# Decay products, norm spacing and tile loads in a conditioned hybrid decoder step

## The chip, the cores and the metric

The kernel runs on one core of one Trainium2 chip. The metric is the device time of one execution in microseconds (us), lower is better. Five engines share the work: TensorE (PE in the profile, matmuls, with its weight loads shown as PEld), VectorE (DVE), ScalarE (ACT), GpSimd (POOL) and SyncE (SP), which issues nearly all transfers. Every engine carries out its own list of instructions in order, and waits on semaphores for the others.

## The reference

One inference step of a two-layer decoder trunk, for a prompt of 1024 tokens and for 8 decoded tokens, with a model width of 1024. Every sub-layer has the same frame:

```
h = h + gate(c) * F(rmsnorm(h) * (1 + scale(c)) + shift(c))
```

`c` is a conditioning vector; scale, shift and gate come from a product with it. Layer 0 mixes with a gated linear recurrence (8 heads of 128 by 128 state, decay `f` per key channel and token), then has a SwiGLU feed-forward block of hidden width 2816:

```
q, f_raw, i, g = split(xn @ w_in, 4)
f = lb + (1 - lb) * sigmoid(f_raw);  k = 1 - f;  v = i
S_t = diag(f_t) S_(t-1) + k_t v_t^T;  o_t = q_t S_t
mix = (rmsnorm(o) * gnorm * silu(g)) @ w_o
```

Then one shared key and value projection is made from a norm of the residual stream. Layer 1 mixes with sliding-window attention (window 128, 16 query heads on 4 shared heads, sinks and a relative bias) and has a second feed-forward block. A last norm gives the output; the recurrent state and the key and value windows are outputs too.

## The kernel before, in words

Activations lie transposed, with the channels on the 128 partitions and 1032 tokens (1024 of the prompt and 8 decoded ones) along the free dimension, in 8 tiles of 128 channels. A product is made with float32 operands split in a high and a low part (three matmuls: high by high, high by low, low by high; L283 to L285). Tokens are cut into three chunks of 344 columns (`G3`) or four chunks of 258 (`G4`). The weights come by the SP queue into three `raw` buffers of 128 by 1024, are split by ScalarE (L182) and GpSimd (L185) into a ring of 8 halves, and `ws.next()` issues the loads of the units that follow within a look-ahead of six halves.

The order of instructions on each engine is not the order of the program. A planner takes instructions by priority, which is their place in the program, as soon as by its own estimate their inputs and a buffer are ready; one that is ready early can come ahead of others that were written earlier. `tc.keep_in_program_order(i)` adds one edge of order and no wait: `i` comes behind the instruction that was written before it for the same engine. Most SBUF tiles share one pool (`c4`) of 34 slots.

**The recurrence** (`hgrn_core`, one call a head). The decayed scores of a token block are built by doubling, at blocks of 1, 2, 4, 8, 16, 32 and 64 tokens. For each level TensorE makes 64 small matmuls of keys by queries (L1041; the two largest levels have lines of their own), and `double` on VectorE scales the second half of every block of queries (L1062) and the first half of the keys (L1063) with the decay of the other half, copies the level's scores under a mask (`take`, L1055), and multiplies the decays of neighbouring blocks (L1067) for the next level: 512 products on each partition at the first level, then 256, down to 8. L1062 and L1063 of one level must be done before L1041 of the next, and must themselves wait for their own level's L1041, which reads what they overwrite. L1067 reads and writes only the decays. `run` interleaves the core of one head with the projections of the next in the program, so large matmuls (L283 to L285) lie between the levels; L1003 and L1005 prepare the decays of the next head on VectorE.

**The norms.** The output projection of each mixer (`wo_second`) makes 8 products for each 258-column chunk; VectorE adds each to the residual stream (L842), ScalarE squares it, VectorE or GpSimd add the squares (L786). When a chunk is complete, a generator (`then`) is queued: `finish` merges the squares (L799), lets some steps pass, sums over the partitions with small matmuls (L712), makes the reciprocal root on VectorE with Newton steps (L543 to L552) and a diagonal tile (L718), lets some steps pass, broadcasts the root over the partitions with a matmul (L727) and copies it (L728). `apply_steps` scales (L807), modulates (ScalarE, L827) and splits (L834, L835) the normed activations. `step()` runs after every product and moves the queued generators on; a step with `LAG` costs nothing itself. After the last chunk, the steps come after the products of the feed-forward block, 24 matmuls each, and `need(x, c)` runs steps until a chunk is ready. The shared keys' norm (`ToKV`) does the same beside the last group of the first feed-forward block, in chunks of 344 columns.

**The feed-forward block** (`ffn`) makes the hidden tiles 0 to 21 and stores each to memory (`act_out`, L1510), most of them with a seven-product scheme whose 28 input tiles fill the pool. For the second matrix the hidden tiles are read back in groups: `hidden(j0, n)` loads n of them (L1517), casts the high part on ScalarE (L1518) and makes the low part on GpSimd and VectorE in turn (L1519). The first group has two tiles, the others four. The loads of the second group (tiles 2 to 5) are written after the products of the first group, and so after the `ws.next()` calls that issue weight loads (L195).

Of the kernel before, what the change touches and what calls it, by code (L numbers as in the profile page):

```python
# [12 lines left out]
ALU = mybir.AluOpType  # L13
# [40 lines left out]
G3, G4 = Grid(344), Grid(258)  # L54
# [3 lines left out]
def bc(ap, axis, n):  # L58
    u = ap.unsqueeze(axis)
    shape = list(u.shape)  # L60
    shape[axis] = n
    return u.to_broadcast(shape)
# [3 lines left out]
def trunk_kernel(  # L66
# [40 lines left out]
    pe, act, dve, pool, sp = nc.tensor, nc.scalar, nc.vector, nc.gpsimd, nc.sync  # L107
# [10 lines left out]
    def nm(s):  # L118
        uid[0] += 1
        return f"{s}_{uid[0]}"  # L120

    def big(dt=F32, cols=TOK, parts=P):
        return p4.tile([parts, cols], dt, tag="c4", name=nm("c4"))
# [11 lines left out]
    def axp():  # L135
        return pp.tile([P, 512], F32, tag="ax", name=nm("ax"), bufs=4)

    def small(shape, tag, bufs=2, dt=F32):
        return sm.tile(shape, dt, tag=tag, name=nm(tag), bufs=bufs)
# [266 lines left out]
    for kk in range(4):  # L406
        t = big(cols=1024)
        wa[0].append(first_half(2 * kk, 0, t))
        t = big(cols=1024)
        wa[0].append(first_half(2 * kk + 1, 0, t))  # L410
    ws.ahead(3)
    for k in range(4):
        t = big(cols=1024)
# [126 lines left out]
    def newton(y, ms, n, parts, tag):  # L540
        t = small([P, 12], tag + "t")[:, :n]
        tv, yv = t[:parts], y[:parts]
        dve.tensor_scalar(  # L543
            tv.bitcast(I32), ms.bitcast(I32), 1, None, op0=ALU.logical_shift_right
        )
        dve.tensor_scalar(
            yv.bitcast(I32), tv.bitcast(I32), -1, MAGIC, op0=ALU.mult, op1=ALU.add
        )
        for _ in range(3):
            dve.scalar_tensor_tensor(tv, yv, -0.5, yv, op0=ALU.mult, op1=ALU.mult)  # L550
            dve.tensor_tensor(tv, tv, ms, op=ALU.mult)
            dve.scalar_tensor_tensor(yv, tv, 1.5, yv, op0=ALU.add, op1=ALU.mult)  # L552
# [4 lines left out]
    def queue(g):  # L557


        later.append([g, next(g) == LAG])  # L560
# [119 lines left out]
    class Norm:  # L680
# [20 lines left out]
            for i in range(2):  # L701
                dve.tensor_reduce(self.acc[i][:, T:TOK], v[:, i], axis=AX.X, op=ALU.add)

        def finish(self, c):
            g = self.g
            s, n, w = g.all(c), g.nq, g.w
            self.merge(c)
            for _ in range(3):
                yield LAG
            ps = axp()  # L710
            for j in range(n):
                pe.matmul(ps[:Q, j : j + 1], self.sums(c, j), ones[:, 0:1], start=True, stop=True)  # L712
            ms = small([P, 12], "nms")
            y = small([P, 12], "ny")
            dve.tensor_scalar(ms[:Q, :n], ps[:Q, :n], 1.0 / D, EPS, op0=ALU.mult, op1=ALU.add)
            newton(y[:, :n], ms[:Q, :n], n, Q, "n")
            dg = small([P, W], "w", 6)[:, :w]
            dve.tensor_tensor(  # L718
                dg[:Q].rearrange("p (j q) -> p j q", j=n),
                bc(ident[:Q, :Q], 1, n),  # L720
                bc(y[:Q, :n], 2, Q),
                op=ALU.mult,
            )
            for _ in range(4):
                yield LAG
            ps = axp()
            pe.matmul(ps[:, :w], ones[:Q, :], dg[:Q], start=True, stop=True)  # L727
            act.copy(self.R[:, s], ps[:, :w])  # L728
# [119 lines left out]
    def residual_dec(tdec):  # L848
        dve.tensor_tensor(hd, hd, tdec, op=ALU.add)


    N = Norm()
# [34 lines left out]
    for half in range(2):  # L887
# [5 lines left out]
            op=ALU.mult,  # L893
# [115 lines left out]
    def hgrn_core(hh):  # L1009
# [6 lines left out]
        for half in range(2):  # L1016
            ps = axp()
            for j in range(4):
                c = 4 * half + j
# [37 lines left out]
        def double(M, pl, off, done=None):  # L1057
            nb = T // (2 * M)
            q4 = QP.rearrange("p (n two m) -> p n two m", two=2, m=M)
            k4 = KS.rearrange("p (n two m) -> p n two m", two=2, m=M)  # L1060
            p3 = pl.rearrange("p (n two) -> p n two", two=2)
            dve.tensor_tensor(q4[:, :, 1, :], q4[:, :, 1, :], bc(p3[:, :, 0], 2, M), op=ALU.mult)  # L1062
            dve.tensor_tensor(k4[:, :, 0, :], k4[:, :, 0, :], bc(p3[:, :, 1], 2, M), op=ALU.mult)  # L1063
            if done:
                take(*done)
            nxt = f[:, off : off + nb]
            dve.tensor_tensor(nxt, p3[:, :, 0], p3[:, :, 1], op=ALU.mult)  # L1067
            return nxt, off + nb

        psv = level(0)  # L1070
# [45 lines left out]
        for half in range(2):  # L1116
            ps = axp()
            for j in range(4):
                c = 4 * half + j
# [6 lines left out]
        for half in range(2):  # L1126
# [4 lines left out]
            for j in range(4):  # L1131
                c = 4 * half + j
# [25 lines left out]
        for half in range(2):  # L1158
            ps = axp()
            po.append(ps)  # L1160
            for j in range(4):
                c = 4 * half + j
                s = slice(c * P, (c + 1) * P)
                o = ps[:, j * P : (j + 1) * P]
# [3 lines left out]
            for j in range(4):  # L1168
                c = 4 * half + j
# [25 lines left out]
        for half in range(2):  # L1195
# [4 lines left out]
                op=ALU.mult,  # L1200
# [4 lines left out]
        for half in range(2):  # L1205
            ps = axp()
            for j in range(4):
                c = 4 * half + j
# [119 lines left out]
    def wo_second(o, gate, m, back, beside=iter(())):  # L1328
        tdec = small([P, KT, NB], "tdec", 2)
        us = [ws.next() for _ in range(4)]  # L1330
        st = res[-1]
        N = StackNorm(st)
        x = Quads()

        def then(c):
            st.move(back, [c], False)
            yield from N.finish(c)
            yield LAG
            yield from N.apply_steps(c, m, x)

        for c in range(G4.n):
            for n in range(KT):
                wo_product(us[n // 2], o, c, n, gate, tdec, G4, anyp)
                N.square(c, n)
                step()
                if c and ((c - 1) * KT + n) % 2 == 0:
                    next(beside, None)
            if c == G4.last:
                residual_dec(tdec)
                N.square_dec()  # L1350
            queue(then(c))
        for _ in beside:
            pass
        return x, st
# [64 lines left out]
    def ffn(l, x, st, hs, norm, aside=None):  # L1419

        gff = 48 * l + 40
        act_out = dp.tile([NF, P, TOK], F32, name=f"ff{l}")
# [87 lines left out]
            sp.dma_start(act_out[j], sg)  # L1510


        def hidden(j0, n, engines=(pool, dve)):
            o = Rows(n)
            for k, (xh, xl) in enumerate(o.t):
                t = big()
                sp.dma_start(t, act_out[j0 + k])  # L1517
                act.copy(xh, t)  # L1518
                engines[k % 2].tensor_tensor(xl, t, xh, op=ALU.subtract)  # L1519
            return o  # L1520
# [14 lines left out]
            seven_products(j, back if j == NF - 1 else None)  # L1535

        o = ready.pop()
        tdec = small([P, KT, NB], "tdec", 2)
        us = [ws.next() for _ in range(2)]
        for c in range(NCH):  # L1540
# [5 lines left out]
                residual(ps, c, n, gff, tdec)  # L1546
        residual_dec(tdec)
        for j0 in range(2, NF - 4, 4):
            o = hidden(j0, 4)
            tdec = small([P, KT, NB], "tdec", 2)  # L1550
            for np_ in range(4):
                u = ws.next()
                for c in range(NCH):
                    for n in (2 * np_, 2 * np_ + 1):
                        wo_product(u, o, c, n, gff, tdec)
            residual_dec(tdec)
        last = norm()
        o = hidden(NF - 4, 4)
# [19 lines left out]
    o = mixed(osc, 0)  # L1578
# [4 lines left out]
    o = mixed(osc, 1)  # L1583
# [6 lines left out]
    class ToKV(StackNorm):  # L1590
# [12 lines left out]

        def then(self, c):
            self.st.move(hsc, [c], False)
            yield from self.finish(c)
            yield LAG
            yield from self.apply_steps(c, 2, self.x, keep=True)

# [21 lines left out]
    for a in range(2):  # L1631
        t = big(cols=T)
# [257 lines left out]
    o = mixed(asc, 0)  # L1890
# [15 lines left out]
    o = mixed(asc, 1)  # L1906
# [137 lines left out]
```

## Time and profile before

| | us |
|---|---|
| median of 3 runs (2546.59 to 2551.95) | 2549.77 |
| the profiled execution | 2554.92 |
| its span, first to last instruction | 2553.1 |
| TensorE busy | 2481.1 |
| VectorE busy | 1370.6 |
| ScalarE busy | 877.9 |
| GpSimd busy | 777.0 |

The mean granted clock of TensorE is 0.988. A row of the waits names the engine and line that waited, then the one that ended the wait, the microseconds in total, how often, and the longest. A row of a timeline has the start in us, the duration, the engine, the line, what is written and read with its shape, the count of merged instructions, and in brackets the idle time of the engine ahead of it and what ended it. A row of grouped instructions has the count, the busy time in us and the mean of one in ns, and the idle time ahead. A row of a stretch has its bounds and length, the busy time of PE, PEld, DVE, ACT and POOL, then the granted clock, the busy share of the DMA engines and GB/s. A row of the chain of waits has start, duration and what it was.

### The profile page before, as it was taken

How to read it: one execution, taken by the hardware profiler on the slowest of the kernel's cores; microseconds unless marked ns; L12 is line 12 of the kernel's file. 1: busy time of each engine (PE TensorE's matmuls, PEld its weight loads, DVE VectorE, ACT ScalarE, POOL GpSimd, SP SyncE). 2: the span in 40 equal slices, each digit the busy share in tenths (PEclk: the TensorE clock that was granted, in tenths of full speed). 3: DMA queues.
4: the chain of work that ended last, by engine and by line, in shares of the span. 5: the costliest groups of instructions: out<-in, count | busy, mean ns of one | idle time of the engine just before them, and what ended most of it. 6: DMA issues, size and time to landing. Idle time of an engine off the chain costs nothing.

```text
span 2553.1 us, 52217 instructions
## 1 busy us (share of the span) xinstructions
PE 2481.1 (97%) x21579; PEld 2355.2 (92%) x21579; DVE 1370.6 (54%) x3117; ACT 877.9 (34%) x1929; POOL 777.0 (30%) x577
## 2 busy tenths in 40 slices
PE   7999999999999999999999999999899999999998
PEld 4988999997889999999999997878899999999998
DVE  5544544565584554655443735567845555554336
ACT  4322322231353332333311555454633333332112
POOL 1211211220324443543432221202234444444321
PEclk9999999999999999999999999999999999999999
DMA  9555222129952223225421321433222222254201
GB/s 318 182 181 168 71 77 69 62 82 293 294 168 84 75 77 122 80 76 190 166 83 45 105 55 59 148 93 108 75 75 84 75 76 75 84 182 166 83 25 67
DMA packets 314495, 293.41 MB, mean 115 GB/s; under 512 B 28617, under 2 KB 291674, under 8 KB 314226
## 3 DMA queue, kind: packets, MB, share of 16 engines
q1 hardware_dynamic: 313856, 289.86, 35.1%
q8 instruction: 170, 2.79, 0.4%
q14 instruction: 67, 0.55, 0.1%
q10 hardware_dynamic: 402, 0.22, 0.0%
HBM read 231.27 MB, written 63.99 MB: 116 GB/s over the span
## 4 chain that ended last, share of the span: by engine, by line
PE 88%; DVE 5%; DMA 4%; issue 2%; SPq 1%; POOL 1%; ACT 0%; DVEq 0%; POOLq 0%
PE mm L283 20%; PE mm L285 19%; PE mm L284 19%; PE ax L283 6%; PE ax L285 6%; PE ax L284 6%; PE ax L473 2%; PE ax L1790 1%; PE ax L1861 1%; DMA c<-in_w_ada_dram 1%; PE ax L1847 1%; PE ax L1041 1%; DVE c L1067 1%; DMA c<-ff 1%; PE ax L1130 1%
## 5 line engine op out<-in xcount | busy, mean ns | idle before, releaser
L185 POOL TENSOR_TENSOR wu<-raw,wu 128x512 fp32r<-128x512 f32 x460 | 618.4, 1351 | 1303.2 <-ACT wu L182 1111.2
L283 PE MATMUL mm<-c,wu 128*128 128x344 f32 (+1 forms) x2096 | 675.0, 323 | 11.9 <-ACT c L1518 5.4
L284 PE MATMUL mm<-c,wu 128*128 128x344 f32 (+1 forms) x2096 | 664.1, 317 | 3.1 <-POOL c L1519 2.0
L285 PE MATMUL mm<-c,wu 128*128 128x344 f32 (+1 forms) x2096 | 663.8, 317 | 0.0
L182 ACT CAST wu<-raw 128x512 fp32r<-128x512 f32 x460 | 283.3, 620 | 622.9 <-PE mm L285 281.3
L283 PEld LDWEIGHTS mm<-c,wu 128*128 128x128 f32 x2096 | 399.6, 191 | 26.7 <-issue 10.2
L283 PE MATMUL mm<-xq,wu 128*128 128x258 f32 x1448 | 412.0, 285 | 1.0 <-ACT wu L182 1.0
L285 PE MATMUL mm<-xq,wu 128*128 128x258 f32 x1448 | 410.9, 284 | 0.8 <-POOL wu L185 0.8
L284 PE MATMUL mm<-xq,wu 128*128 128x258 f32 x1448 | 410.1, 283 | 0.0
L284 PEld LDWEIGHTS mm<-c,wu 128*128 128x128 f32 x2096 | 400.9, 191 | 8.1 <-POOL c L1519 2.8
L285 PEld LDWEIGHTS mm<-c,wu 128*128 128x128 f32 x2096 | 400.2, 191 | 4.6 <-issue 4.5
L285 PE MATMUL ax<-xq,wu 128*128 128x258 f32 x1064 | 300.9, 283 | 0.0
L284 PE MATMUL ax<-xq,wu 128*128 128x258 f32 x1064 | 300.9, 283 | 0.0
L283 PE MATMUL ax<-xq,wu 128*128 128x258 f32 x1064 | 300.8, 283 | 0.0
L284 PEld LDWEIGHTS mm<-xq,wu 128*128 128x128 f32 x1448 | 276.0, 191 | 1.3 <-issue 1.2
L283 PEld LDWEIGHTS mm<-xq,wu 128*128 128x128 f32 x1448 | 275.0, 190 | 2.0 <-ACT wu L182 1.2
L285 PEld LDWEIGHTS mm<-xq,wu 128*128 128x128 f32 x1448 | 275.0, 190 | 1.1 <-POOL wu L185 1.1
L842 DVE SCALAR_TENSOR_TENSOR hs<-mm,ada,hs 128x344 f32<-128x344 f32 (+3 forms) x228 | 120.3, 533 | 180.1 <-PE mm L285 166.0
L284 PEld LDWEIGHTS ax<-xq,wu 128*128 128x128 f32 x1064 | 201.9, 190 | 0.0
L283 PEld LDWEIGHTS ax<-xq,wu 128*128 128x128 f32 x1064 | 201.5, 189 | 0.0
L285 PEld LDWEIGHTS ax<-xq,wu 128*128 128x128 f32 x1064 | 200.9, 189 | 0.0
L842 DVE SCALAR_TENSOR_TENSOR c<-mm,ada,c 128x344 f32<-128x344 f32 (+1 forms) x132 | 75.1, 572 | 117.1 <-PE mm L285 116.3
(323 smaller groups left out, 3576.2 us busy)
## 6 DMA issues: line engine op xcount, KB each, us to landing
c<-in_w_ada_dram SPq DMA_DIRECT2D x96, 512.0 KB
raw<-in_w_ffn_in_dram SPq DMA_DIRECT2D x152, 256.0 KB
ff<-c SPq DMA_DIRECT2D x44, 516.0 KB
c<-ff SPq DMA_DIRECT2D x44, 516.0 KB
raw<-in_w_ffn_out_dram SPq DMA_DIRECT2D x44, 512.0 KB
raw<-in_w_in_a_dram SPq DMA_DIRECT2D x32, 512.0 KB
hs<-hs SPq DMA_DIRECT2D x16, 516.0 KB
out_dram<-c SPq DMA_DIRECT2D x16, 512.0 KB
```

Of the source, the lines that this page charges most:

```text
L182: i = act.copy(u[:, 0, :], src)
L185: eng.tensor_tensor(u[:, 1, :], src, u[:, 0, :], op=ALU.subtract)
L283: pe.matmul(ps, wh, xh, start=first, stop=False)
L284: pe.matmul(ps, wh, xl, start=False, stop=False)
L285: pe.matmul(ps, wl, xh, start=False, stop=last)
L473: pe.matmul(ada_ps[q][32 * j : 32 * j + 32, 256 * i : 256 * i + 256], cT[:, k, :], u[i][:, j, :], start=(k == 0 and i == 0), stop=(k == KT ...
L842: dve.scalar_tensor_tensor(hc, ps[:, : g.pl[c]], ada[:, gate + n, 0:1], hc, op0=ALU.mult, op1=ALU.add)
L1041: pe.matmul(ps[32 * j : 32 * j + 32, c * 32 : (c + 1) * 32], KS[:, t0 : t0 + 32], QP[:, t0 : t0 + 32], start=True, stop=True, tile_positio ...
L1067: dve.tensor_tensor(nxt, p3[:, :, 0], p3[:, :, 1], op=ALU.mult)
L1130: pe.matmul(ps[:, j * P : (j + 1) * P], kt[:, s], vt[:, s], start=True, stop=True)
L1790: pe.matmul(psv[hf][:, gi, s0:256], q[2 * gp + gi][r, tb * P : (tb + 1) * P], kT[a][r, (tb - 1) * P + s0 : (tb + 1) * P], start=True, stop ...
L1847: pe.transpose(ps[:, g * P : (g + 1) * P], L[:, g, sb * P : (sb + 1) * P], ident)
```

## The change

Three places are edited. In `double`, the product of neighbouring decays (L1067) is kept in program order, behind the VectorE instruction written before it, which is the masked copy of its own level, or the scaling of the keys at the two largest levels.

`finish` takes the number of steps ahead of the sum and ahead of the broadcast as arguments. They were 3 and 4 everywhere. They become 3 and 8 in the two output projections for all chunks but the last, 2 and 4 there for the last chunk, and 3 and 5 for the norm of the shared keys.

`hidden` issues all its loads ahead of the casts. The second group's call moves ahead of the first group's `ws.next()` calls, with each of its four loads kept in program order on the SP queue, the first of them behind the store of the last hidden tile.

```diff
-        def finish(self, c):
+        def finish(self, c, before, after):
             g = self.g
             s, n, w = g.all(c), g.nq, g.w
             self.merge(c)
-            for _ in range(3):
+            for _ in range(before):
                 yield LAG
             ps = axp()
...
-            for _ in range(4):
+            for _ in range(after):
                 yield LAG
...
             nxt = f[:, off : off + nb]
-            dve.tensor_tensor(nxt, p3[:, :, 0], p3[:, :, 1], op=ALU.mult)
+            tc.keep_in_program_order(dve.tensor_tensor(nxt, p3[:, :, 0], p3[:, :, 1], op=ALU.mult))
...
             st.move(back, [c], False)
-            yield from N.finish(c)
+            yield from N.finish(c, *((3, 8) if c < G4.last else (2, 4)))
             yield LAG
...
-        def hidden(j0, n, engines=(pool, dve)):
+        def hidden(j0, n, engines=(pool, dve), pin=False):
             o = Rows(n)
+            ts = []
+            for k in range(n):
+                ts.append(big())
+                i = sp.dma_start(ts[k], act_out[j0 + k])
+                if pin:
+                    tc.keep_in_program_order(i)
             for k, (xh, xl) in enumerate(o.t):
-                t = big()
-                sp.dma_start(t, act_out[j0 + k])
+                t = ts[k]
                 act.copy(xh, t)
...
         o = ready.pop()
+        o4 = hidden(2, 4, pin=True)
         tdec = small([P, KT, NB], "tdec", 2)
         us = [ws.next() for _ in range(2)]
...
         for j0 in range(2, NF - 4, 4):
-            o = hidden(j0, 4)
+            o = hidden(j0, 4) if j0 > 2 else o4
...
             self.st.move(hsc, [c], False)
-            yield from self.finish(c)
+            yield from self.finish(c, 3, 5)
             yield LAG
```

## The prediction

> **What bounds the kernel now.** I read the page first, then TensorE's waits, then each long wait's place in the timelines of TensorE, VectorE and the SP queue.
>
> ```profile
> PE 2481.1 (97%) x21579; PEld 2355.2 (92%) x21579; DVE 1370.6 (54%) x3117; ACT 877.9 (34%) x1929; POOL 777.0 (30%) x577
> ...
> PE ax L1041 <- DVE c L1063: 14.7, 6, 2.9
> PE ax L727 <- DVE w L718: 9.8, 4, 6.1
> ...
> PE mm L283 <- ACT c L1518: 5.4, 2, 4.5
> ...
> PE mm L284 <- POOL c L1519: 2.0, 2, 1.4
> ```
>
> TensorE is busy for 97% of the span and its matmuls follow each other in one fixed order, so a microsecond in which it idles is a microsecond of the end, wherever it stands. The four waits shown are 31.9 us, nearly half of its idle time, and each is named by a line that the change touches: the decay levels (L1041), a norm's broadcast (L727), the hidden tiles (L1518, L1519).
>
> **Part 1, decay products.** TensorE around the third head's levels:
>
> ```profile
> 246.18 0.76 PE L1041 MATMUL ax<-c,c 128*32 128x32 f32 x64
> ...
> 247.14 0.32 PE L284 MATMUL mm<-c,wu 128*128 128x344 f32 x1
> ...
> 250.60 0.32 PE L285 MATMUL mm<-c,wu 128*128 128x344 f32 x1
> 250.85 0.76 PE L1041 MATMUL ax<-c,c 128*32 128x32 f32 x64
> ...
> 256.60 0.85 PE L1041 MATMUL ax<-c,c 128*32 128x32 f32 x64 [2.89 <-DVE c L1063]
> ...
> 257.84 0.49 PE L284 MATMUL mm<-c,wu 128*128 128x344 f32 x1
> ...
> 260.42 0.36 PE L284 MATMUL mm<-c,wu 128*128 128x344 f32 x1
> ```
>
> Levels come every 4.67 us (246.18 to 250.85) until one waits 2.89 us for the second scaling of the level before (L1063). VectorE shows why:
>
> ```profile
> 248.53 5.99 DVE L1067 TENSOR_TENSOR c<-c 128x512 f32<-128x512 f32 x7
> ...
> 255.17 0.69 DVE L1062 TENSOR_TENSOR c<-c,c 128x512 f32<-128x512 f32 x1
> ```
>
> All seven products of the head, which need only one another, run together for 5.99 us, and L1062 of the next level stands behind them. Only the first is needed by then. Pinned, each product follows the copy of its own level, so six of the seven leave this place and go one by one into later levels. They are as many as before; no instruction and no wait is added.
>
> What is late next? One level costs, at most:
>
> ```profile
> L1063 DVE TENSOR_TENSOR c<-c,c 128x512 f32<-128x512 f32 x56 | 49.4, 882 | 0.0
> L1062 DVE TENSOR_TENSOR c<-c,c 128x512 f32<-128x512 f32 x56 | 45.5, 813 | 99.4 <-PE ax L1041 78.6 <-PE ax L1087 13.3 <-PE ax L1108 7.3
> L1055 DVE COPY_PREDICATED acc<-masks,ax 128x256 f32<-128x256 int32 x40 | 17.7, 442 | 0.0
> ...
> L1067 DVE TENSOR_TENSOR c<-c 128x512 f32<-128x512 f32 x8 | 10.1, 1265 | 0.0
> ...
> L1003 DVE TENSOR_SCALAR c<-c,omlb,lb 128x1032 f32<-128x1032 f32 x8 | 7.2, 903 | 3.8 <-ACT c L995 3.8
> ```
>
> ```profile
> 249.25 2.12 DVE c L1067
> ```
>
> A level's chain is TensorE 0.76, then 0.81 + 0.88 + 0.44 + 1.27 = 3.40 us on VectorE: 4.16 us, under the pitch of 4.67, with the widest product in it; the other six have shorter means. The longest of them on the chain of waits, the second one of this bunch, took 2.12 us; a level with that is at 5.01 and 0.34 late. L1003 and its sister L1005 can still step in once a head: 0.90 us for the first by its mean over eight heads.
>
> The wait has a second price, the granted clock after it (third column from the right):
>
> ```profile
> 256.60:261.60 5.00, 5.00 (x82) 4.94 (x83) 2.45 (x5) 0.45 (x1) 0.00 (x0) 0.66 0.11 32
> 322.60:328.60 6.00, 5.98 (x81) 5.94 (x82) 2.47 (x5) 0.45 (x1) 0.00 (x0) 0.50 0.04 12
> ...
> 522.90:527.90 5.00, 4.93 (x81) 4.90 (x82) 2.52 (x5) 0.45 (x1) 0.00 (x0) 0.66 0.01 3
> 1446.40:1450.40 4.00, 3.91 (x23) 3.75 (x24) 4.00 (x7) 2.85 (x5) 0.77 (x1) 1.00 0.38 115
> ```
>
> These are the stretches behind the five waits of 2.7 to 2.9 us (first, second and last of five; the third and fourth read 0.66 over 5 us and 0.50 over 6 us as well): the clock is at half for a while. After a wait of 1.40 us (last row) it is full. The lost share is 5 x 0.34 + 6 x 0.50 + 1.7 + 3.0 + 1.7 = 11.1 us, that is 22.2 us at half clock. There ten starts lie 2.58 / 9 = 0.287 us apart (257.84 to 260.42) against 3.46 / 22 = 0.157 (247.14 to 250.60), so 22.2 x (1 - 0.157 / 0.287) = 10.1 us are lost. Part 1 is worth 14.7 + 10.1 = 24.8 in full. Bounds: 11 (six heads keep a wait of 1.4, L1003's 0.90, the 0.34 above and a little more, with half the slow clock: 24.8 - 8.4 - 5.0) to 24.8. I take 22.5, near the full price since the chain of 4.16 fits, less about 0.3 a head for L1003.
>
> [...]
>
> **Part 2, the broadcast of a norm.** Sum and broadcast are TensorE instructions; between them VectorE makes the root in twelve small steps. The number of products between them goes from 4 to 8 (both mixers' norms, all chunks but the last), to 5 (the shared keys' norm), and stays 4 for a last chunk, whose sum moves one product earlier. No instruction is added. The two worst places:
>
> ```profile
> 1811.53 0.28 PE L283 MATMUL mm<-c,wu 128*128 128x258 f32 x1
> 1812.25 0.28 PE L283 MATMUL mm<-xq,wu 128*128 128x258 f32 x1
> ...
> 1821.29 1.20 PE L727 MATMUL ax<-w,ones 86*128 86x258 f32 x2 [6.13 <-DVE w L718]
> ```
>
> ```profile
> 1820.73 0.42 DVE L718 TENSOR_TENSOR w<-ident,ny 86x258 f32<-86x258 f32 x1
> ...
> 1824.27 0.41 DVE L799 TENSOR_TENSOR sq<-sq 128x250 f32<-128x250 f32 x1
> ```
>
> ```profile
> 1821.30:1827.30 6.00, 6.00 (x26) 5.82 (x27) 3.93 (x8) 5.33 (x10) 0.95 (x1) 0.51 0.25 85
> ```
>
> A 258-wide matmul takes 0.72 / 6 = 0.12 us (1811.53 to 1812.25). In the second mixer the third chunk's broadcast waits 6.13 us; the clock behind it costs 6 x 0.49 x 0.91 = 2.7 (0.91 is 10.1 / 11.1). Four steps later, one product and three feed-forward steps of 24 matmuls, it comes behind 72 of these: 1812.25 + 8.6 = 1820.9, against L718's end at 1821.15, so this wait is gone. But the delay on VectorE isn't. The last chunk's sum moves from behind 72 of these matmuls to behind 48 (one step fewer), so it is due at 1812.25 + 5.8 = 1818.0, and its merge (L799) ends at 1824.68. Some of that lag goes, since the second chunk's scaling also moves behind: two or three of its steps, 1.2 us each by L807 in the same stretch. I put the merge at about 1822: a new wait of some 4 us, with 1.5 of slow clock. So of 0.96 (the second chunk's wait there) + 6.13 + 2.7 = 9.8 about 4.5 stay. In the first mixer the wait of 1.30 goes and the last sum meets its merge about 1.5 early: nothing. In the shared keys' norm:
>
> ```profile
> 1446.49 0.82 PE L727 MATMUL ax<-w,ones 86*128 86x344 f32 x2 [1.40 <-DVE w L718]
> ...
> 1457.73 0.77 PE L712 MATMUL ax<-ones,sq 128*86 128x1 f32 x8 [0.99 <-DVE sq L799]
> ```
>
> The next sum already waits 0.99 us for its merge, so what the broadcast gives back is asked for eleven microseconds later: nothing again. Part 2: 4.5, bounds -5.5 (all three last sums wait, with slow clock) to 9.8 + 1.3 + 1.4 = 12.5.
>
> **Part 3, hidden tiles of the second group.** SP issues in order:
>
> ```profile
> 2284.66 0.45 SPq L1517 DMA_DIRECT2D c<-ff  x1
> 2298.00 0.38 SPq L195 DMA_DIRECT2D raw<-in_w_ffn_out_dram  x1
> ```
>
> ```profile
> 2282.91 7.99 DMA c<-ff
> ...
> 2298.44 5.68 DMA c<-ff
> ...
> 2304.14 1.06 ACT c L1518
> ...
> 2305.27 2.38 POOL c L1519
> ```
>
> ```profile
> 2305.24 1.23 PE L283 MATMUL mm<-c,wu 128*128 128x344 f32 x3 [4.47 <-ACT c L1518]
> ```
>
> ```profile
> 2305.20:2311.20 6.00, 5.31 (x17) 4.87 (x18) 1.23 (x1) 2.11 (x2) 4.47 (x2) 0.50 0.44 176
> ```
>
> Two of the four tiles go out early; the third stands 13.3 us behind a weight load that waits for its buffer. Ahead of that load it goes out at about 2286; with 8 us of flight, 1.06 of cast and 2.38 on POOL it is there at 2297.5, before TensorE asks at 2305.24 - 4.47 = 2300.8. The early weight loads that now follow move by three or four issues of 0.45 and as many transfers; TensorE needs them only after the unit before, 72 matmuls x 0.157 = 11.3 us, which covers that. Eight tile buffers are held earlier; the seven-product factors have given theirs up by then. Worth: 4.47 + 0.65 + 6 x 0.5 x 0.91 = 7.8 in this layer; in the other, waits of 0.98 and 1.39 without slow clock. Full 10.2, and at least 5 if casts of late tiles now stand on ACT ahead of weight casts. I take 9.5.
>
> **Sum.** 22.5 + 4.5 + 9.5 = 36.5. The profiled execution took 2554.92 us (span 2553.1), 5.15 above the median 2549.77. 2554.92 - 36.5 = 2518.4, on the median's scale 2513.
>
> **Rivals.**
> - The wait moves to the sums: every last chunk's sum waits long enough for slow clock, part 2 is -5.5: gain 26.5, 2523. For it: the 0.99 row, and L799 at 1824.27. Against: the planner may place the sums later by its own estimate.
> - The levels stay tight: part 1 gives its lower bound of 11, gain 25, 2525. For it: the 2.12 product. Against: 4.16 under 4.67.
> - The slow stretches are not tied to the waits: 36.5 without 10.1, 2.7 and 2.7, with the 1.5 of the new wait back: gain 22.5, 2527. Against: the clock rows.
> - The change doesn't do what it says: the planner leaves the order at the three places: 2550, no change. Against: the pin is an edge of order, and more steps move the broadcast in program order.
> - Slower: VectorE becomes the bound of every level. With 2.12 for each product and one operation like L1003 (0.90) in each level the chain is 0.76 + 0.81 + 0.88 + 0.44 + 2.12 + 0.90 = 5.91, 1.24 over the pitch; 5 levels x 7 heads make 43.4, against the 24.8 saved: part 1 is -18.6, the whole 4.6 slower, 2554. It decides from a mean product of about 2 us; the mean of the widest is 1.27.
>
> **Numbers.** Forecast 0.57 (its own range 2504 to 2522), sums 0.16, tight levels 0.10, untied clock 0.04, no effect 0.05, slower 0.08. About 0.2% (5 us) can be told from no change. Faster 0.87, same 0.05, slower 0.08. The low end has all three parts in full, 47.5: 2502, and 1 for chance; the high end has the lower bounds of parts 1 and 2 and a little over half of part 3, 11 - 5.5 + 6 = 11.5: 2538.
>
> **What would show it.** Part 1: no wait of L1041 on L1063 near 2.7 us, L1067 as single rows between L1055 and L1062, clock 1.00 through the heads. Part 2: no L727 wait on L718, but L712 waiting on L799 near 1818. Part 3: four c<-ff issues in a row ahead of the weight load, no wait on L1518. I am wrong if L1041's waits persist at 1 us or more in most heads, or if new waits of the same size stand where these were.

## The result, and the profile after

The changed kernel took 2525.5 us in the median (2524.4 to 2529.6) against 2548.2 us for the kernel before in the same comparison (2544.0 to 2552.0). The ratio is 0.9915, with a 95% interval of 0.9901 to 0.9929: 18 to 25 us faster, where 36.5 were forecast. The profiled executions, 2554.92 before and 2529.57 after, differ by 25.35 us.

In the changed file, L712, L718 and L727 are L714, L720 and L729; L799 is L801; L842 is L844; L1003, L1005 and the level's lines L1041, L1055, L1062, L1063 and L1067 are each two higher; L1517 to L1519 have become L1520, L1525 and L1526. The page's engine line, and TensorE's waits as before (who waited, for whom, us in total, times, longest):

```profile
PE 2469.5 (98%) x21579; PEld 2346.0 (93%) x21579; DVE 1366.9 (54%) x3117; ACT 878.7 (35%) x1929; POOL 797.3 (32%) x577
...
PE ax L714 <- DVE sq L801: 8.8, 5, 5.8
PE ax L1043 <- DVE c L1065: 8.1, 7, 1.8
...
PE ax L729 <- DVE w L720: 1.6, 1, 1.6
```

The instructions are as many as before. The waits for the levels are 8.1 us instead of 14.7, those for a broadcast 1.6 instead of 9.8, those for the second group's hidden tiles are gone. But the sums of the norms (L714), which waited 0.99 us before, now wait 8.8.

**The decay levels.** VectorE, then GpSimd, then TensorE in timelines of the changed kernel at the third head, where the wait was 2.89 us, and the stretch behind:

```profile
247.11 0.45 DVE L1057 COPY_PREDICATED acc<-masks,ax 128x256 f32<-128x256 int32 x1
247.44 0.68 DVE L1069 TENSOR_TENSOR c<-c 128x512 f32<-128x512 f32 x1
250.36 1.63 DVE L1005 TENSOR_SCALAR c<-c,omlb,lb 128x1032 f32<-128x1032 f32 x1 [2.24 <-ACT c L946]
251.91 1.77 DVE L1064 TENSOR_TENSOR c<-c,c 128x512 f32<-128x512 f32 x1
253.60 0.68 DVE L1065 TENSOR_TENSOR c<-c,c 128x512 f32<-128x512 f32 x1
```

```profile
248.30 1.90 POOL L1125 TENSOR_TENSOR c<-c,c 128x1024 f32<-128x1024 f32 x1 [13.78 <-DVE c L1069]
250.15 2.97 POOL L185 TENSOR_TENSOR wu<-raw,wu 128x512 fp32r<-128x512 f32 x2
```

```profile
254.42 0.75 PE L1043 MATMUL ax<-c,c 128*32 128x32 f32 x64 [1.80 <-DVE c L1065]
```

```profile
254.50:259.50 5.00, 5.00 (x136) 4.75 (x137) 2.79 (x7) 0.45 (x1) 0.00 (x0) 1.00 0.35 101
```

The product (L1069) is single and stands between the copy and the next scaling, as announced. The wait has not gone: it is 1.80 us here and 0.7 to 1.4 at six more places. Two things make it. L1005 (L1003 of the kernel before), which prepares the next head, starts at 250.36, just ahead of the level's first scaling (L1064). And that scaling takes 1.77 us where its sister behind it (L1065) takes 0.68, while GpSimd makes low parts of weights (L185). At the fourth to seventh head L1005 takes 0.80 to 0.83 us, the scaling 1.78 to 1.79 again, and the waits are 1.02 to 1.12. The clock behind the wait is 1.00, and none of the seven waits has half clock behind it. One stretch at half clock is left in the heads, 3.41 us from 570.95 on, behind 3.76 us in which TensorE waited for nothing that the profile shows; the kernel before had one of 3.41 us at 581.35.

**The norms.** TensorE's two longest waits for a sum, in the shared keys' norm and at the last chunk of the second mixer, and the stretches behind them:

```profile
1436.10 0.77 PE L714 MATMUL ax<-ones,sq 128*86 128x1 f32 x8 [1.65 <-DVE sq L801]
...
1807.16 0.74 PE L714 MATMUL ax<-ones,sq 128*86 128x1 f32 x4 [5.83 <-DVE sq L801]
```

```profile
1436.70:1441.70 5.00, 5.00 (x25) 5.00 (x25) 4.54 (x16) 3.52 (x6) 0.00 (x0) 0.66 0.24 54
...
1807.20:1813.20 6.00, 6.00 (x28) 5.92 (x29) 3.77 (x9) 0.93 (x2) 0.00 (x0) 0.50 0.31 90
```

The broadcast's wait of 6.13 us has become a sum's wait of 5.83, with the same half clock behind it (6 x 0.50 x 0.91 = 2.7). VectorE and GpSimd ahead of the second sum, from the third chunk's root to the last chunk's merge (L801):

```profile
1789.60 1.26 DVE L546 TENSOR_SCALAR ny<-nt 86x3 int32<-86x3 int32 x1
1790.78 0.46 DVE L844 SCALAR_TENSOR_TENSOR hs<-mm,ada,hs 128x250 f32<-128x250 f32 x1
1791.16 0.94 DVE L550 SCALAR_TENSOR_TENSOR nt<-ny 86x3 f32<-86x3 f32 x1
...
1792.13 0.16 DVE L551 TENSOR_TENSOR nt<-nt,nms 86x3 f32<-86x3 f32 x1
...
1795.58 0.93 DVE L551 TENSOR_TENSOR nt<-nt,nms 86x3 f32<-86x3 f32 x1
...
1802.70 2.29 DVE L837 TENSOR_TENSOR xq<-hs,xq 128x1032 fp32r<-128x1032 f32 x1
1804.91 1.73 DVE L788 TENSOR_TENSOR sq<-sq,sq 128x500 f32<-128x500 f32 x1
...
1806.70 0.41 DVE L801 TENSOR_TENSOR sq<-sq 128x250 f32<-128x250 f32 x1
```

```profile
1789.39 2.70 POOL L185 TENSOR_TENSOR wu<-raw,wu 128x512 fp32r<-128x512 f32 x2 [1.14 <-ACT wu L182]
1792.98 3.52 POOL L185 TENSOR_TENSOR wu<-raw,wu 128x512 fp32r<-128x512 f32 x2 [0.90 <-ACT wu L182]
...
1801.65 4.46 POOL L185 TENSOR_TENSOR wu<-raw,wu 128x512 fp32r<-128x512 f32 x2
```

A step of the root on 86x3 numbers takes 0.16 us when it is alone (1792.13), and 0.93 to 1.26 beside L185. Those that are stretched end with an instruction of GpSimd: 1791.16 + 0.94 = 1792.10 and 1789.39 + 2.70 = 1792.09; 1795.58 + 0.93 = 1796.51 and 1792.98 + 3.52 = 1796.50. L844, which reads one input from the matmuls' accumulators (mm), took 0.46 us there (1790.78) and 0.47 where GpSimd had nothing to do (1797.28). Nearer the sum, L837 takes 2.29 us and L788 1.73; in the ninth kernel below, where GpSimd does nothing beside them, they take 1.22 and 0.67.

**The hidden tiles.** The SP queue of the changed kernel:

```profile
2258.59 0.32 SPq L1512 DMA_DIRECT2D ff<-c  x1
2259.01 3.23 SPq L1520 DMA_DIRECT2D c<-ff  x4
2262.60 1.22 SPq L195 DMA_DIRECT2D raw<-in_w_ffn_out_dram  x2
```

Four loads go out behind the last store and ahead of the weights. TensorE has no wait left on their casts (L1525) or low parts (L1526).

**Where the 25 us came from.** In the levels 14.7 - 8.1 = 6.6 of waiting and the 10.1 of half clock. In the hidden tiles 5.4 + 2.0 of waiting and 2.7 of half clock, 10.1. In the norms, waiting and half clock were 0.99 + 9.8 + 2.7 = 13.5; they are 8.8 + 1.6 + 2.7 + 1.5 (5 x 0.34 x 0.91, at the shared keys) = 14.6, a loss of 1.1. Together 16.7 + 10.1 - 1.1 = 25.7, against 25.35 between the two profiled executions. That they agree so closely is partly luck: at two places that the change doesn't touch, the changed kernel's execution has 6.8 us more at half clock (3.41 at 1536.92, and 6.83 at 1649.56 against 3.41 at 1670.20), about 3 us by the prediction's price, which the sum leaves out.

### The profile page after: what moved, and what is told of

Its sections match the earlier page's. It is cut to its first block, busy times and chain, and to the rows that moved or that the text cites. A ratio compares the mean times of both kernels' runs of the same rounds, so it can differ in the third digit from the quotient of the medians.

```text
span 2527.8 us, 52251 instructions
## 1 busy us (share of the span) xinstructions
PE 2469.5 (98%) x21579; PEld 2346.0 (93%) x21579; DVE 1366.9 (54%) x3117; ACT 878.7 (35%) x1929; POOL 797.3 (32%) x577
## 4 chain that ended last, share of the span: by engine, by line
PE 89%; DVE 5%; DMA 2%; issue 2%; SPq 1%; ACT 0%; POOL 0%; DVEq 0%; POOLq 0%; ACTq 0%
PE mm L283 20%; PE mm L285 20%; PE mm L284 20%; PE ax L283 6%; PE ax L284 6%; PE ax L285 6%; PE ax L473 2%; PE ax L1798 1%; PE ax L1869 1%; PE ax L1043 1%; PE ax L1855 1%; DVE c L1064 1%; PE ax L1132 1%; PE ax L1169 1%; DVE hs L809 1%
## 5 line engine op out<-in xcount | busy, mean ns | idle before, releaser
L185 POOL TENSOR_TENSOR wu<-raw,wu 128x512 fp32r<-128x512 f32 x460 | 626.2, 1368 | 1354.8 <-ACT wu L182 1118.7
L283 PEld LDWEIGHTS mm<-c,wu 128*128 128x128 f32 x2096 | 395.6, 189 | 20.0 <-issue 10.3
L285 PEld LDWEIGHTS mm<-c,wu 128*128 128x128 f32 x2096 | 395.6, 189 | 6.2 <-issue 4.1
L284 PEld LDWEIGHTS mm<-c,wu 128*128 128x128 f32 x2096 | 396.2, 189 | 4.3 <-issue 3.4
L844 DVE SCALAR_TENSOR_TENSOR hs<-mm,ada,hs 128x344 f32<-128x344 f32 (+3 forms) x228 | 120.5, 532 | 183.8 <-PE mm L285 170.8
L844 DVE SCALAR_TENSOR_TENSOR c<-mm,ada,c 128x344 f32<-128x344 f32 (+1 forms) x132 | 74.9, 571 | 111.3 <-PE mm L285 110.6
```

Source lines behind the costliest of these rows:

```text
L185: eng.tensor_tensor(u[:, 1, :], src, u[:, 0, :], op=ALU.subtract)
L283: pe.matmul(ps, wh, xh, start=first, stop=False)
L284: pe.matmul(ps, wh, xl, start=False, stop=False)
L285: pe.matmul(ps, wl, xh, start=False, stop=last)
L844: dve.scalar_tensor_tensor(hc, ps[:, : g.pl[c]], ada[:, gate + n, 0:1], hc, op0=ALU.mult, op1=ALU.add)
```

## The experiments

The numbers in brackets behind a time are the ratio to the kernel before and its 95% interval. Kernels 1 to 4 have one measurement of the kernel before in common (2549.75 us), kernels 5 to 8 one (2547.66), 9 to 11 one (2549.88), the twelfth one of its own (2547.76).

### One part alone

The first kernel has the pinned product and nothing else of the change:

```diff
-            dve.tensor_tensor(nxt, p3[:, :, 0], p3[:, :, 1], op=ALU.mult)
+            tc.keep_in_program_order(dve.tensor_tensor(nxt, p3[:, :, 0], p3[:, :, 1], op=ALU.mult))
```

> Only the decay products are kept in program order; the norms and the hidden tiles are as before. Theory A (the three parts act apart, each by the idle time and half clock it removes in the two profiles): the waits of the decay levels fall from 14.7 to about 8 us and the half clock behind them (about 10 us) goes, so 16 us less: 2532. Rival B (the full price of the recorded prediction, 22.5): 2526. Rival C (the saving in the changed kernel comes from a general reordering and not from this edit): within 5 us of 2548.

Measured: 2533.5 us (0.9942, 0.9929 to 0.9955), that is 11 to 18 us. The waits of the levels are still 6.7 us in six places, the longest 1.6 (waits of TensorE), and the clock behind the longest is full:

```profile
PE ax L1041 <- DVE c L1063: 6.7, 6, 1.6
```

```profile
256.00:261.00 5.00, 5.00 (x145) 4.75 (x131) 2.60 (x6) 0.45 (x1) 0.00 (x0) 1.00 0.34 98
```

So part 1 is 15, not the 22.5 of the forecast: of the idle time about half stayed.

The second kernel has the norms' step counts alone:

```diff
...
-            yield from N.finish(c)
+            yield from N.finish(c, *((3, 8) if c < G4.last else (2, 4)))
...
-            yield from self.finish(c)
+            yield from self.finish(c, 3, 5)
```

> Only the steps ahead of the norms' sums and broadcasts are changed. Theory A: what the broadcasts stop waiting for is waited for at the last chunk's sum, 13.5 us of waits and half clock before against some 14.7 after, so no gain: 2548 to 2550, with a wait of L714 on L801 near 6 us in the second mixer. Rival B (recorded prediction, 4.5 us): 2543.

Measured: 2551.8 us (1.0011, 1.0001 to 1.0022), 0.3 to 5.6 us slower, 2.8 in the middle. Its waits on the norms are those of the full change:

```profile
PE ax L714 <- DVE sq L801: 8.9, 5, 6.0
...
PE ax L729 <- DVE w L720: 1.7, 1, 1.7
```

The third has the hidden tiles' loads alone:

```diff
...
         o = ready.pop()
+        o4 = hidden(2, 4, pin=True)
         tdec = small([P, KT, NB], "tdec", 2)
...
-            o = hidden(j0, 4)
+            o = hidden(j0, 4) if j0 > 2 else o4
```

> Only the second group's hidden tiles are loaded ahead of the weights. Theory A: the waits on the third tile, 7.5 us, and 2.7 of half clock go: 10 us less, 2538. Rival B (the loads in front delay the weights, half is given back): 2543.

Measured: 2535.6 us (0.9949, 0.9932 to 0.9966), 9 to 17 us faster; the forecast's 9.5 lies in it. The waits for the tiles are gone here too. The profile shows something else. The heads are those of the kernel before, with five waits of 2.4 to 2.9 us, but in the stretches behind them the clock is at half only three times:

```profile
255.20:260.20 5.00, 4.99 (x81) 4.96 (x82) 2.45 (x5) 0.45 (x1) 0.00 (x0) 0.66 0.18 53
321.30:326.30 5.00, 5.00 (x83) 4.94 (x84) 2.44 (x5) 0.45 (x1) 0.00 (x0) 0.68 0.06 17
387.10:392.10 5.00, 4.99 (x127) 4.75 (x128) 2.46 (x5) 0.45 (x1) 0.00 (x0) 1.00 0.06 16
451.65:456.65 5.00, 5.00 (x128) 4.75 (x130) 2.45 (x5) 0.45 (x1) 0.00 (x0) 1.00 0.04 11
515.80:520.80 5.00, 4.96 (x83) 4.93 (x84) 2.48 (x5) 0.45 (x1) 0.00 (x0) 0.68 0.03 8
```

Two of these waits on TensorE:

```profile
321.30 1.08 PE L1043 MATMUL ax<-c,c 128*32 128x32 f32 x64 [2.71 <-DVE c L1065]
...
387.12 0.75 PE L1043 MATMUL ax<-c,c 128*32 128x32 f32 x64 [2.71 <-DVE c L1065]
```

So the same wait costs half clock in one place and none in another; the last section has what the clock records say of it.

The three parts alone give 14.8 - 2.8 + 13 = 25, at the upper end of the 18 to 25 of the change as a whole: no sign that they hinder each other.

### The change without its norms

```diff
-            yield from N.finish(c, *((3, 8) if c < G4.last else (2, 4)))
+            yield from N.finish(c, 3, 4)
...
-            yield from self.finish(c, 3, 5)
+            yield from self.finish(c, 3, 4)
```

> The changed kernel with the steps of the norms as before (3 and 4 everywhere). Theory A: part 2 is worth nothing or costs a microsecond, so this is as fast as the changed kernel or faster: 2522 to 2526, with the broadcast's wait of about 6 us back at the third chunk of the second mixer. Rival B (part 2 saves 4.5): 2530.

Measured: 2525.2 us (0.9906, 0.9893 to 0.9919), as fast as the change. The broadcast waits 9.8 us again, 6.2 at its worst. Part 2 has moved a wait from one place of the norm to another.

### A later last sum, and one instruction moved off VectorE

The fifth kernel gives the last chunk of the mixers three more steps ahead of its sum, so that it meets its merge:

```diff
-            yield from N.finish(c, *((3, 8) if c < G4.last else (2, 4)))
+            yield from N.finish(c, *((3, 8) if c < G4.last else (5, 3)))
```

> The changed kernel, but the last chunk of each mixer's norm waits 5 steps ahead of its sum and 3 ahead of its broadcast (2 and 4 in the change). Theory A (the last sum stands ahead of its merge on VectorE): the sum comes behind 120 feed-forward matmuls, 14 us, past the merge's end, so the wait of 5.8 us and the half clock behind it go: 8 us less than the changed kernel, about 2517. Rival B (VectorE is simply too late there, and the time is paid at the next chunk's activations): L283 or L284 waits for L837 or L844 by some 5 us, 2523 to 2526.

Measured: 2527.9 us (0.9917, 0.9903 to 0.9931), no gain over the change. The wait of 5.83 is gone, but the same chunk's broadcast has a new one, at a place that neither expectation named:

```profile
1819.31 1.13 PE L729 MATMUL ax<-w,ones 86*128 86x258 f32 x2 [3.62 <-DVE w L720]
```

The sixth moves the instruction that steps in ahead of the levels' scaling to ScalarE, with the steps of the change:

```diff
-        dve.tensor_scalar(f, f, omlb[:, hh : hh + 1], lb[:, hh : hh + 1], op0=ALU.mult, op1=ALU.add)
+        act.activation(f, f, AF.Identity, scale=omlb[:, hh : hh + 1], bias=lb[:, hh : hh + 1])
```

> The changed kernel with the first operation of the next head's decay (L1005 of the changed kernel) on ScalarE, as an activation with scale and bias, instead of VectorE; the same values. Theory A (what is left of the levels' waits, 8.1 us, is this operation stepping in ahead of the scaling): they fall under 2 us, 6 us less, about 2519. Rival B (it is GpSimd, which doubles the scaling itself from 0.7 to 1.8 us): the waits fall by half at most, 2521 to 2523.

Measured: 2526.0 us (0.9908, 0.9894 to 0.9923). The time doesn't tell it from the change, and lies above both expectations (2519, and 2521 to 2523). The waits for the scaling fall from 8.1 us to 3.6, with 1.7 of new waits for ScalarE: about 2.8 us, between the two expectations.

The seventh has both edits, and the eighth gives the shared keys' norm later sums as well (4 and 6 steps, for the last chunk 4 and 5):

> The edits of the two runs above together. They touch stages that lie a thousand microseconds apart, so theory A of both has them add: 14 us less than the changed kernel, about 2511. If they don't add, 2517 or above.

> The run above, and in the shared keys' norm 4 steps ahead of the sum and 6 ahead of the broadcast (4 and 5 for the last chunk) instead of 3 and 5. Theory A (each wait there is a distance too short): the waits of 1.6 and 1.65 us and 1.6 of half clock go, 4 us less than the run above: 2507. Rival B (VectorE is the bound of that stage and the wait moves on to the activations): no change, 2511.

Measured: 2521.9 us (0.9896, 0.9880 to 0.9911) and 2521.5 us (0.9893, 0.9877 to 0.9909). Both fall short of the 2511 and 2507 that theory A had for them. In the seventh the last chunk's broadcast still waits 3.9 us, the longest of TensorE's waits for a norm. In the eighth the waits of the shared keys' norm are gone, but the products wait for the scaled activations instead:

```profile
1423.12 0.43 PE L284 MATMUL mm<-xt,wu 128*128 128x344 f32 x1 [2.03 <-DVE xt L837]
```

As in the fourth and fifth, a step count doesn't remove the lag, it only names the instruction that waits for it. The lag itself has to be found.

### GpSimd taken away from the norm and from the heads

The rows of the changed kernel point at GpSimd. In the ninth kernel the low parts of six weight tiles, those that are made beside the second mixer's norm, are not made by GpSimd; in the eleventh those of the recurrence's input weights. ScalarE writes zeros in their place, so both kernels leave a part of those products out:

```diff
-        eng.tensor_tensor(u[:, 1, :], src, u[:, 0, :], op=ALU.subtract)
+        if low:
+            eng.tensor_tensor(u[:, 1, :], src, u[:, 0, :], op=ALU.subtract)
+        else:
+            act.activation(u[:, 1, :], src, AF.Identity, scale=0.0, bias=0.0)
...
```

> The changed kernel, with the low part of the weights of the first three hidden tiles in the second feed-forward block set to zero by ScalarE instead of being made by GpSimd (L185); that part of the product is left out. In the changed kernel the small root steps beside the second mixer's norm end when a GpSimd instruction ends (0.9 to 1.3 us instead of 0.16), and the last sum waits 5.8 us. Theory A (GpSimd beside VectorE makes the lag): the small steps are back at 0.16 us, the scaling of the activations (2.29 us at its longest) at 1.2, the wait of 5.8 us is under 2 and the half clock behind it (2.65 us) goes: 6 to 8 us less than the changed kernel, near 2519. Theory B (the number of VectorE instructions ahead of the last merge makes it): the wait stays above 4 us, and the time within 2 us of the changed kernel.

Measured: 2517.2 us (0.9876, 0.9853 to 0.9899), an interval just below that of the change. The file is four lines longer ahead of the norm, so L551, L801 and L714 are L555, L805 and L718. VectorE, GpSimd, TensorE and the stretch behind:

```profile
1786.08 0.15 DVE L555 TENSOR_TENSOR nt<-nt,nms 86x3 f32<-86x3 f32 x1
...
1795.75 0.40 DVE L805 TENSOR_TENSOR sq<-sq 128x250 f32<-128x250 f32 x1
```

```profile
1791.50 1.30 POOL L792 TENSOR_TENSOR sq<-sq,sq 128x500 f32<-128x500 f32 x1 [14.57 <-ACT sq L790]
```

```profile
1796.20 0.62 PE L718 MATMUL ax<-ones,sq 128*86 128x1 f32 x6 [0.28 <-DVE sq L805]
```

```profile
1796.00:1802.00 6.00, 5.80 (x48) 5.74 (x49) 4.91 (x18) 3.35 (x6) 0.00 (x0) 1.00 0.31 90
```

The one row of GpSimd is all that it does from 1777 to 1796. The steps take 0.15 us, the last sum waits 0.28 us instead of 5.83, and the clock behind it is full. VectorE has the same work ahead of the merge as in the changed kernel, and goes through it, from the third chunk's first root step to the merge's end, in 14.7 us (1781.44 to 1796.15) instead of 19.2 (1787.95 to 1807.11). So the lag came with GpSimd's work, as theory A had it.

> The changed kernel, with the low part of the recurrence's input weights set to zero by ScalarE instead of being made by GpSimd (L185); that part of the product is left out. Theory A (GpSimd makes most of what is left of the level waits): L1064 takes 0.69 us at the level that waited (1.77 in the changed kernel), and the waits of L1043 for L1065 fall from 8.1 us to under 4.5. Theory B (L1005 stepping in ahead of the scaling makes it, GpSimd or not): seven waits near 1 us remain, 6 to 8 us in all. The time as a whole is less of a guide here, since ScalarE takes 64 more operations of 0.6 us in the heads: by A about 4 us less than the changed kernel, by B the same.

Measured: 2520.8 us (0.9886, 0.9860 to 0.9912). Waits of TensorE, then VectorE at the third head:

```profile
PE ax L1047 <- DVE c L1069: 2.4, 2, 1.4
```

```profile
245.64 2.00 DVE L1068 TENSOR_TENSOR c<-c,c 128x512 f32<-128x512 f32 x1 [3.11 <-PE ax L1047]
...
250.11 0.82 DVE L1009 TENSOR_SCALAR c<-c,omlb,lb 128x1032 f32<-128x1032 f32 x1 [0.94 <-ACT c L950]
250.84 0.69 DVE L1068 TENSOR_TENSOR c<-c,c 128x512 f32<-128x512 f32 x1
251.45 0.69 DVE L1069 TENSOR_TENSOR c<-c,c 128x512 f32<-128x512 f32 x1
```

L1009 (L1005 of the changed kernel) still steps in ahead of the scaling, but takes 0.82 us instead of 1.63, the scaling takes 0.69 instead of 1.77, and two waits with 2.4 us are left of seven with 8.1. So GpSimd makes most of what part 1 had left over; with L1005 still in the way, five of the seven waits went with GpSimd's L185. The first row is stretched by a GpSimd instruction that stays in this kernel (L1125 of the changed one):

```profile
245.19 1.90 POOL L1129 TENSOR_TENSOR c<-c,c 128x1024 f32<-128x1024 f32 x1 [66.54 <-DMA c<-vsc]
```
The time agrees, but its interval overlaps that of the change, so the rows carry this.

### What a faster kernel would have

The tenth kernel is the fourth with the scaling of the forget gate on ScalarE; norms as before the change:

> Parts 1 and 3 of the change and the forget gate's scaling (L1005) on ScalarE; the norms keep their old 3 and 4 steps. Theory A (the norm spacing is worth nothing, whatever stands beside it): the 24 us of parts 1 and 3 and the 2 us of the moved scaling, near 2522, and the broadcast's wait of 6 us back in the profile. Theory B (the norm spacing is worth its 4.5 us and was hidden in the comparison by chance): 2526 to 2528, later than the kernel that has a late last sum and the scaling on ScalarE (0.9896) by 4 us or more.

Measured: 2518.9 us (0.9881, 0.9861 to 0.9901), with the broadcast's wait of 6.2 us in its profile. It is no slower than the seventh, whose norms were spaced. Part 2 is worth nothing here either.

The twelfth is the tenth with the ninth's finding put to use: VectorE makes the low parts of those six tiles, in full.

```diff
...
-            ntile(w_ffn_in[l], j * P)
-            ntile(w_ffn_in[l], DFF + j * P)
+            ntile(w_ffn_in[l], j * P, (pool, dve)[l])
+            ntile(w_ffn_in[l], DFF + j * P, (pool, dve)[l])
```

> The kernel with parts 1 and 3 and the forget gate's scaling on ScalarE (0.9881), in which VectorE instead of GpSimd makes the low parts of the weights of the first three hidden tiles in the second feed-forward block: 12 instructions of 128x512, some 0.68 us each, all computed in full. Theory A (GpSimd beside VectorE stretched the root's small steps): the steps of the second mixer's root take 0.16 us, its third broadcast waits under 2 us instead of 6.2 without any change of the norm's step counts, and 5 to 8 us go: a ratio near 0.985. Theory B (VectorE's own list is the limit): the 8 us of added work on VectorE stand in the same place, the broadcast or a scaling waits 4 us or more, and the ratio stays at 0.988 or above.

Measured: 2513.1 us (0.9862, 0.9834 to 0.9890), 28 to 42 us faster than the kernel before and outside the interval of the change; against the tenth alone the intervals overlap. The place where the broadcast waited 6.2 us, on TensorE, VectorE and GpSimd:

```profile
1796.27 0.70 PE L730 MATMUL ax<-w,ones 86*128 86x258 f32 x2 [1.00 <-DVE w L721]
```

```profile
1793.86 0.15 DVE L551 SCALAR_TENSOR_TENSOR nt<-ny 86x3 f32<-86x3 f32 x1
...
1794.04 1.26 DVE L552 TENSOR_TENSOR nt<-nt,nms 86x3 f32<-86x3 f32 x1
```

```profile
1794.02 1.27 POOL L789 TENSOR_TENSOR sq<-sq,sq 128x500 f32<-128x500 f32 x1 [16.42 <-ACT sq L787]
```

With the norm's old step counts and twelve instructions more on VectorE the wait is 1.00 us. The 1.00 that is left has the same cause: one step of the root starts 0.02 us behind the one GpSimd instruction there is, and both end at 1795.3.

## Why the prediction was right or wrong

Faster was right, and the 2525 that came out lies in the whole range; it lies outside the forecast's own range of 2504 to 2522. The sum was too large, in two of its terms.

By the signs that the prediction set itself, it was wrong in two parts: TensorE still waits 1.0 us or more for the levels in six of eight heads, and a wait of 5.83 us stands where one of 6.13 was. That the time falls on the 2525 of the rival with tight levels is chance, since that rival has 11 for part 1 and 4.5 for part 2.

**Part 1, 22.5 forecast, 15 (alone) to 16.7 (by the rows) measured.** The mechanism was right: single products behind the copies, no wait near 2.7 us, full clock behind the level waits. The step that failed is "near the full price since the chain of 4.16 fits, less about 0.3 a head for L1003". The chain was summed from means over 56 instructions, and a mean over all places is not the duration at the place that decides: at the third head the scaling takes 1.77 us (0.69 with GpSimd away), and L1003 (L1005 of the changed kernel) steps in with 1.63, not with its mean of 0.90. Together that is 1.80 of wait there and 8.1 over seven heads, 1.2 a head where 0.3 was allowed. Of the bound of 11, the waits were in it at about this size; the half clock that it kept did not come. The quoted means (0.81 for the scaling of the queries, 0.69 where it is alone) already held the slow cases, spread over all levels.

**Part 2, 4.5 forecast, -1 by the rows and -2.8 alone.** That the wait goes to the last sum was foreseen, with "some 4 us, with 1.5 of slow clock"; it was 5.83 with 2.7. The failed step is "Some of that lag goes, since the second chunk's scaling also moves behind": the lag doesn't depend much on the order of VectorE's list, it is largely made of instructions stretched by GpSimd, and these stayed. In the shared keys' norm "nothing again" missed a wait of 1.65 with half clock. The rival that the wait moves to the sums is what happened, at a little over half of the 10 us by which it differs from the forecast.

**Part 3, 9.5 forecast, 10.1 by the rows and 13 (9 to 17) alone.** Right, step by step: the loads go out together ahead of the weights, nothing else became late.

**The half clock.** It was priced as a sure consequence of a wait of 2.7 us. The rival of slow stretches not tied to the waits is refuted, since they went with the waits; but the price of 10.1 is only what that execution showed, and that it came behind all five waits was luck. With the tiles alone, three of five such waits had it (0.66 to 0.68 over 5 us, against 1.00 behind the other two). The price was read from an execution that took 5.15 us more than the median, and then taken off the median as well.

The slower rival needed a product of 2 us in each level. In the changed kernel only the widest product of a head took as long, at two of eight heads and beside GpSimd; where they stood alone the products took 0.68 us and less. The 2.12 us of that rival was GpSimd's too: in the kernel before, at the third head, the first and widest of the seven products took 0.68 us, the second 2.10 beside GpSimd's L1123, the third and fourth 1.26 and 1.20 beside L185, and the last three 0.17 to 0.19. So most of the 5.99 us of that bunch, which the prediction put down to the products running together, came with GpSimd's work: the three stretched ones took 4.56 together, and 0.89 at the same head of the changed kernel (0.41 at 254.53, 0.27 at 257.02, 0.21 at 261.43), with no GpSimd beside them.

## What to carry to other kernels

Before moving a wait, find out what makes the engine behind it late: a wait that is only spaced out appears at the next instruction that needs the same engine, as four kernels here show (the change, and the second, fifth and eighth). Price a chain by the durations at the place that decides, not by means, and look at what GpSimd does in those microseconds. Small VectorE steps on a critical path were better kept away from GpSimd's work here, even at the cost of twelve more instructions on VectorE: the broadcast behind them waited 1.00 us instead of 6.2.

## What the runs showed of the hardware

**VectorE's instructions took longer beside GpSimd's.** A root step of 0.16 us took 0.93 to 1.26 and ended together with GpSimd's instruction to 0.02 us, in the changed kernel and in the twelfth. A scaling of 128x512 took 1.77 instead of 0.69 and ended 0.56 us behind L185 (253.68 and 253.12); the one of 2.00 us in the eleventh ended 0.55 behind GpSimd's end at 247.09. Both are one pattern in the rows with two inputs: the instruction held up ends at GpSimd's recorded end, plus its own time alone, less 0.13 to 0.14 (253.12 + 0.69 - 0.13 = 253.68; 247.09 + 0.69 - 0.14 = 247.64; 1792.09 + 0.15 - 0.14 = 1792.10). L844, with an input from the accumulators, kept its 0.46 us beside L185. L546 and L1005, which have one wide input each, were stretched as well, to 1.26 and 1.63 us (at their shortest 0.16 and 0.80). By what means GpSimd holds VectorE up, no run here shows.

**A wait of 1.65 us brought half clock, and one of 2.71 didn't.** In the changed kernel the clock was at half for a while after 1.65 us at 1436.10 (0.66 over 5 us), and full after 1.80 us at 254.42 (1.00 over 5 us). With the tiles alone, behind 2.71 us it was at half (321.30, 0.68 over 5 us) and full (387.12, 1.00 over 5 us) in one execution. So the length of a wait alone didn't decide it.

The clock records of the kernel before and of the changed one show more, though no run was made to test it. In the kernel before, the five stretches behind the levels begin at 257.08, 321.94, 390.20, 455.06 and 523.32, which lie 19, 20, 19 and 20 times 3.413 us apart, and each lasts 3.41 or 6.83 us. In the changed kernel those at 570.95, 994.21 and 1437.94 lie 124 and 130 times 3.413 us apart. Each of the two executions can be divided into pieces of this length, with the starts of half clock on their bounds, and TensorE's idle time added up in each piece. From 45 us on to 15 us before the end, all 9 pieces at full clock with more than 1.9 us of idle time were followed by half clock, 6 of 9 with 1.4 to 1.9 us, and 1 of 1412 with less, among the small matmuls of the attention (half clock from 1649.56 in the changed kernel). With the tiles alone, divided in the same way, the wait at 321.30 leaves 2.48 us of idle time in one piece; the one at 387.12 is divided into 1.51 and 1.20, and the clock stays full. So in these executions the price of a wait of 2.7 us went with how it lay across such pieces. What decides between 1.4 and 1.9 us is open.
